# Six 512-column products ahead of one gate product in a one-core hybrid attention and RWKV layer

## The chip, the cores and the metric

The kernel runs on one core of a Trainium2 chip. What is measured is the device time of one execution in microseconds (us), and the comparison is between medians of repeated runs. TensorE (PE in the profile) multiplies, VectorE (DVE), ScalarE (ACT) and GpSimd (POOL) work elementwise, and SyncE (SP) issues the transfers. Each engine works through its own queue in order.

## The reference, cut to what matters

One layer over 512 tokens of width 1024: an input projection, a sparse attention (NSA) on half of the mixed width and an RWKV-7 recurrence on the other half, an output projection with residual, and a feed-forward part with squared ReLU. The change stands at the end of the RWKV half, where the normalised state output gets its bonus and is multiplied by a gate:

```python
def rwkv7_mixer(cols, ...):
    ...
    g = jax.nn.sigmoid(xg) @ g2
    ...
    y = wkv7_scan(rh, decay.reshape(B, T, H, N), kh, vh, -kk, kk * ah)
    ...
    y = ((y - mean) * lax.rsqrt(var + GN_EPS)).reshape(B, T, RWKV_WIDTH) * lnx_w + lnx_b
    bonus = jnp.sum(rh * kh * r_k, axis=-1, keepdims=True) * vh
    y = y + bonus.reshape(B, T, RWKV_WIDTH)
    return (y * g).astype(cols.dtype)
```

The matrix `g2` has 128 rows and 512 columns; the kernel holds it as the tile `G2P`, and sigmoid(xg) as `SG`.

## The kernel before

The 512 tokens are cut into four tiles of 128 (index `i`). Python generators stand for streams of work: the input projection (`rw_in`, `rw_v`, `nsa_in`), the RWKV steps of one tile (`rw_prep`, `rw_inv`, `rw_vals`), the recurrence over chunks (`rw_scan`), its output (`rw_outs`, which calls `rw_out(i)`), and the attention of one tile and head group (`attn_scores`, `attn_values`). `merge` takes turns among them by priority and by a modelled clock of its own, and so gives the order in which the program is written. The framework then plans the order of each engine's queue from modelled times (`schedule_with_timeline_sim=True`, line 1429), so instructions of neighbouring streams stand interleaved in the queues, and a plan made with more instructions need not keep the order of the rest.

The products of the input projection and of the feed-forward part go through `mm3` (lines 331 to 334), three products in single-pass form in place of one float32 product. Other products, among them the gate product, are plain float32; the profile records such a product as two TensorE instructions.

Results of TensorE land in PSUM banks. The tag `ps` has one bank, which `rw_out`, `rw_prep` and `rw_vals` share in turn: a tile of that tag can be written only when the reader of the one before is done. `pa` and `pb` have two banks each, `pi`, `pq` and `pz` one.

In `rw_out(i)` (lines 769 to 801) four transposes write `pty` (line 787), ScalarE reads it with scale and bias into `Y1` (line 792), GpSimd adds the bonus (line 794), the gate product of four 128-column pieces writes `pgt` in the same bank (line 797), and VectorE multiplies the two into `YR` (line 799). Around the first tile's gate product stand, on other streams: the triangular inverse of tile 1 (`rw_inv`: lines 694, 702, 712), its products with the state (lines 743, 752, 757), the preparation of tile 2 (`BK` at line 568, `pg` at line 586, read by VectorE at lines 589 and 590), the bonus of tile 1 (`rkp`, line 622) and the attention scores (`pcs` at line 1053, `sc` at line 1075, read by VectorE at lines 1058 and 1079 and by ScalarE at lines 1061 and 1082).

Of the kernel before, what the change touches and what calls it, by code (L numbers as in the profile page):

```python
# [114 lines left out]
def layer(ctx: ExitStack, tc: tile.TileContext, A, cst, out):  # L115
    nc = tc.nc
    PSUM = bass.MemoryType.PSUM
    V, S, G, PE = nc.vector, nc.scalar, nc.gpsimd, nc.tensor

    def bc(ap, shape):  # L120
        return ap.to_broadcast(shape)
# [54 lines left out]
    def at(place, shape, name, dt=F32):  # L176
        size, n = PLACES[place]
        assert int(np.prod(shape[1:])) * 4 <= size
        return up.tile(shape, dt, name=name, tag=place, bufs=n)
# [10 lines left out]
    def small(n, name):  # L190
        return sm.tile([128, n], F32, name=name, tag=name, bufs=1 if n == 32 else 2)
# [12 lines left out]
    ident = identr.bitcast(F32)  # L204
# [82 lines left out]
    def vec(key, j=0, n=1):  # L287
        return VEC[:, VO[key] + j:VO[key] + j + n]
# [10 lines left out]
    def rsqrt(v, n, key, p=128):  # L299

        y = small(n, "rs_y" + key)[0:p]
        G.tensor_tensor(y, v, bc(MH[0:p], [p, n]), op=ALU.pow)
        return y
# [27 lines left out]
    def mm3(o_, l, r, first, last):  # L331
        PE.matmul(o_, l[0], r[0], start=first, stop=False)  # L332
        PE.matmul(o_, l[0], r[1], start=False, stop=False)  # L333
        PE.matmul(o_, l[1], r[0], start=False, stop=last)  # L334

    def norm_T(i, x_, gain, NH_, NL_, place, pool, raw=None):

        ss = small(2, "ss")
        tmp = [at(place, [128, 512], "nt") for _ in range(2)]
        for b in range(2):  # L340
            S.activation(tmp[b], x_[b], AF.Square, scale=1.0 / 32, accum_out=ss[:, b:b + 1])
        vv = small(1, "vv")
        V.scalar_tensor_tensor(vv, ss[:, 0:1], 1e-6, ss[:, 1:2], op0=ALU.add, op1=ALU.add)
        rs = rsqrt(vv, 1, 'n')
        for b in range(2):
            V.scalar_tensor_tensor(tmp[b], x_[b], rs, gain[b], op0=ALU.mult, op1=ALU.mult)
            pt = pool([128, 4, 128], "pt")
            for kk in range(4):
                PE.transpose(pt[:, kk, :], tmp[b][:, kk * 128:(kk + 1) * 128], ident)
            S.copy(NH_[b][:, i], pt)  # L350
            if raw:
                S.copy(raw[b], pt)
            V.tensor_tensor(NL_[b][:, i], pt, NH_[b][:, i].bitcast(F32), op=ALU.subtract)
# [22 lines left out]
    G2P = at('c', [128, 4, 128], "G2P")  # L376
# [66 lines left out]
    def feat_cols(c0, use, halves=False):  # L443

        turn[0] ^= 1
        pas = [(pa_, pb_)[turn[0]]([128, T], "pa") for _ in range(2)]
        W = []
        for a in range(2 if halves else 1):
            i0, i1 = (2 * a, 2 * a + 2) if halves else (0, NT)
            for h in range(4):  # L450
                if a == 0:
                    W.append(piece(c0, h))
                hi, lo = W[h]
                for kk in range(2):
                    k = 2 * h + kk
                    for j in range(2):
                        js = slice(j * 128, (j + 1) * 128)
                        mm3(t4(pas[j])[:, i0:i1], (hi[:, kk, js], lo[:, kk, js]), xk(k, i0, i1), k == 0, k == KD - 1)
                    yield 1.3 * (i1 - i0) / NT, 0.0
        for j in range(2):  # L460
            use(j, pas[j])
# [307 lines left out]
    def rw_out(i):  # L769
        st = ST[i]  # L770
        YY = st['YY']
        mean = small(8, "mean")
        V.tensor_reduce(mean, YY, axis=AX.X, op=ALU.add)
        V.tensor_scalar(mean, mean, 1.0 / 64, None, op0=ALU.mult)
        V.tensor_tensor(YY, YY, bc(mean.unsqueeze(2), [128, 8, 64]), op=ALU.subtract)
        sq = at('o', [128, 8, 64], "sqy")
        S.activation(sq, YY, AF.Square)
        var = small(8, "var")
        V.tensor_reduce(var, sq, axis=AX.X, op=ALU.add)
        V.tensor_scalar(var, var, 1.0 / 64, 64e-5, op0=ALU.mult, op1=ALU.add)  # L780
        rs = rsqrt(var, 8, 'o')
        V.tensor_tensor(YY, YY, bc(rs.unsqueeze(2), [128, 8, 64]), op=ALU.mult)
        yield 0.0, 5.0
        pt = ps([128, 2, 2, 2, 64], "pty")
        for c in range(2):
            for p in range(2):
                PE.transpose(pt[:, c, p].rearrange("p a b -> p (a b)"),
                             YY[:, 4 * c + 2 * p:4 * c + 2 * p + 2, :].rearrange("p a b -> p (a b)"), ident)
        Y1 = at('o', [128, 4, 128], "Y1")
        for p in range(2):  # L790
            for e in range(2):
                S.activation(Y1[:, 2 * p + e, :].rearrange("p (c t) -> p c t", c=2), pt[:, :, p, 1 - e, :],
                             AF.Identity, bias=vec('lnb', 2 * p + e), scale=vec('lnw', 2 * p + e))
        G.tensor_tensor(Y1, Y1, st['ZV'], op=ALU.add)
        pgt = ps([128, 4, 128], "pgt")
        for kt in range(4):
            PE.matmul(pgt[:, kt, :], G2P[:, kt, :], SG[:, i * 128:(i + 1) * 128], start=True, stop=True)
        YR[i] = at('zk', [128, 4, 128], "YR")
        V.tensor_tensor(YR[i], Y1, pgt, op=ALU.mult)
        done['out', i] = 1  # L800
        yield 1.3, 0.0
# [8 lines left out]
    def rw_outs():  # L810
        for i in range(NT):
            yield lambda: ('chain', i) in done
            yield from rw_out(i)
# [22 lines left out]
    def tok_cols(c0, n, use):  # L836

        pas = [(pa_ if i < 2 else pb_)([128, 512], "pa") for i in range(NT)]
        for h in range(4):
            hi, lo = piece(c0, h)  # L840
            for kk in range(2):
                k = 2 * h + kk
                for i in range(NT):
                    mm3(pas[i][:, 0:n], xt(k, i), (hi[:, kk, :], lo[:, kk, :]), k == 0, k == KD - 1)
                    if i % 2:
                        yield 0.7, 0.0
        for i in range(NT):
            use(i, pas[i][:, 0:n])
# [331 lines left out]
    def outproj():  # L1180
        for i, b in OPO:
                yield lambda: ('n', i) in YS and ('r', i) in YS and ('wo', b) in done and all(z in done for z in GATE)
                Y2[i][b] = at(('zv', 'zr')[b], [128, 512], "y2")
                nc.sync.dma_start(Y2[i][b], A['x'][0, i * 128:(i + 1) * 128, b * 512:(b + 1) * 512])
                pa = pa_([128, 512], "pa")
                for k in range(KD):
                    y_ = YS['nr'[k // 4], i]
                    mm3(pa, (y_[0][:, k % 4, :], y_[1][:, k % 4, :]), WO[b, k], k == 0, k == KD - 1)
                V.tensor_tensor(Y2[i][b], Y2[i][b], pa, op=ALU.add)
                yield 5.2, 0.0  # L1190
                done['op', i, b] = 1
# [241 lines left out]
```

## Time and profile before

| | us |
|---|---|
| median of 3 runs | 785.54 |
| lowest and highest of the 3 | 783.43, 785.77 |
| the profiled execution | 783.81 |
| its span, first to last instruction | 781.9 |
| TensorE busy | 759.8 |
| VectorE busy | 511.8 |
| ScalarE busy | 395.6 |
| GpSimd busy | 175.2 |

The span is what the trace shows; 1.9 us of the profiled execution lie outside it. [...] A timeline row gives the start and the length of a group of instructions, their count, and in square brackets the idle time of the engine before them and what ended it. A row of the chain gives the time that a group put on the chain that ended last.

### The profile page before, as it was taken

Reading aid. Unit: us, or ns where it says so; the run is one execution under the profiler, and the core shown is the slowest. Engines: PE = TensorE matmul, PEld = TensorE weight load, DVE = VectorE, ACT = ScalarE, POOL = GpSimd, SP = SyncE. Lnnn points to the kernel's source line nnn. Section 1 sums busy time; section 2 is a strip of 40 time slices with the busy share of each in tenths; the row PEclk is TensorE's granted clock in tenths of the full one; section 3 lists DMA queues with packets and bytes.
Section 4 is the critical chain, followed back from the end, with each engine's and each line's share of the span. In section 5 each row is a group of like instructions: output and inputs, shape, how many; then the busy total and the mean of one; then the engine's idle time right before and its main releaser. Section 6 shows DMA issues by size and latency. Waiting matters only on the chain.

```text
span 781.9 us, 18278 instructions
## 1 busy us (share of the span) xinstructions
PE 759.8 (97%) x7357; PEld 657.5 (84%) x7357; DVE 511.8 (65%) x1157; ACT 395.6 (51%) x928; POOL 175.2 (22%) x176
## 2 busy tenths in 40 slices
PE   7999999999989999999999899999999999999998
PEld 5888888889879877887788899998888999978886
DVE  6444385585586789898755888973334989853333
ACT  7343433345444867888544655673332456653330
POOL 5002032240332353434400152300001323100000
PEclk9999999999985999999999999999999999999999
DMA  7741331111000000120343053233323433133212
GB/s 235 206 133 42 94 84 44 44 29 31 15 16 1 29 3 2 30 57 9 114 149 95 17 146 108 69 104 110 96 92 103 118 102 106 62 122 95 95 54 108
DMA packets 67338, 62.00 MB, mean 79 GB/s; under 512 B 6013, under 2 KB 53299, under 8 KB 67254
## 3 DMA queue, kind: packets, MB, share of 16 engines
q1 hardware_dynamic: 67254, 60.83, 25.9%
q8 instruction: 58, 0.95, 0.5%
q14 instruction: 26, 0.21, 0.1%
HBM read 58.72 MB, written 2.10 MB: 78 GB/s over the span
## 4 chain that ended last, share of the span: by engine, by line
PE 84%; DVE 7%; ACT 4%; DMA 3%; issue 1%; SPq 1%; POOL 0%; DVEq 0%; ACTq 0%; POOLq 0%
PE pa L332 8%; PE pa L333 8%; PE pa L334 8%; PE po L332 7%; PE po L333 7%; PE po L334 7%; PE pw L333 5%; PE pw L334 5%; PE pw L332 5%; PE pg L586 2%; PE sc L1075 2%; DMA wraw<-in_w_out_dram 1%; PE py L757 1%; PE pT L1111 1%; PE pz L681 1%
## 5 line engine op out<-in xcount | busy, mean ns | idle before, releaser
L311 ACT CAST whi<-wraw 128x512 fp32r<-128x512 f32 (+1 forms) x128 | 78.7, 622 | 133.4 <-PE po L333 29.1
L312 DVE TENSOR_TENSOR wlo<-wraw,whi 128x512 fp32r<-128x512 f32 (+1 forms) x120 | 86.7, 725 | 86.1 <-ACT whi L311 80.9
L332 PE MATMUL po<-whi 128*128 128x512 f32 x256 | 100.7, 394 | 1.2 <-DVE cc L1361 1.2
L333 PE MATMUL po<-wlo,whi 128*128 128x512 f32 x256 | 101.0, 395 | 0.0
L334 PE MATMUL po<-whi,wlo 128*128 128x512 f32 x256 | 100.7, 393 | 0.0
L333 PE MATMUL pw<-TT,whi 128*128 128x256 f32 x224 | 63.2, 282 | 0.0
L334 PE MATMUL pw<-TT,wlo 128*128 128x256 f32 x224 | 63.0, 281 | 0.0
L332 PE MATMUL pw<-TT,whi 128*128 128x256 f32 x224 | 62.5, 279 | 0.0
L332 PEld LDWEIGHTS po<-whi 128*128 128x128 f32 x256 | 48.0, 188 | 13.0 <-ACT whi L311 1.6
L334 PEld LDWEIGHTS po<-whi,wlo 128*128 128x128 f32 x256 | 48.1, 188 | 11.4
L333 PEld LDWEIGHTS po<-wlo,whi 128*128 128x128 f32 x256 | 48.0, 188 | 11.0
L332 PE MATMUL pa<-XH,whi 128*128 128x512 f32 (+1 forms) x144 | 53.0, 372 | 1.5 <-ACT XH L350 1.5
L333 PE MATMUL pa<-XL,whi 128*128 128x512 f32 (+1 forms) x144 | 53.7, 374 | 0.0
L334 PE MATMUL pa<-XH,wlo 128*128 128x512 f32 (+1 forms) x144 | 52.9, 370 | 0.0
L1291 POOL TENSOR_TENSOR ws<-wq 128x512 f32<-128x512 f32 x14 | 21.5, 1536 | 138.3 <-DMA wq<-in_w_ff_dram 123.2
L311 ACT CAST whi<-ws 128x512 fp32r<-128x512 f32 x56 | 33.0, 617 | 34.7 <-DVE ws L1296 9.5
L312 DVE TENSOR_TENSOR wlo<-ws,whi 128x512 fp32r<-128x512 f32 x56 | 48.2, 870 | 3.1 <-ACT whi L311 3.0
L1089 POOL TENSOR_SCALAR P<-P,z 128x128 f32<-128x128 f32 (+3 forms) x32 | 36.1, 1138 | 60.8 <-DVE z L1038 28.5
L312 DVE TENSOR_TENSOR wlo<-H,whi 128x512 fp32r<-128x512 f32 x32 | 22.1, 690 | 42.1 <-PE po L333 37.4
L334 PE MATMUL pw<-NH,wlo 128*128 128x256 f32 x168 | 47.0, 280 | 0.0
L333 PE MATMUL pw<-NL,whi 128*128 128x256 f32 x168 | 46.8, 279 | 0.0
L332 PE MATMUL pw<-NH,whi 128*128 128x256 f32 x168 | 46.8, 279 | 0.0
(317 smaller groups left out, 2007.9 us busy)
## 6 DMA issues: line engine op xcount, KB each, us to landing
wraw<-in_w_ff_dram SPq DMA_DIRECT2D x72, 256.0 KB
wq<-in_w_ff_dram SPq DMA_DIRECT2D x56, 256.0 KB
wraw<-in_w_in_dram SPq DMA_DIRECT2D x40, 256.0 KB
wraw<-in_w_in_dram SPq DMA_DIRECT2D x8, 268.0 KB
x<-in_x_dram SPq DMA_DIRECT2D x8, 256.0 KB
y<-in_x_dram SPq DMA_DIRECT2D x8, 256.0 KB
wraw<-in_w_out_dram SPq DMA_DIRECT2D x8, 256.0 KB
wraw<-in_w_out_dram SPq DMA_DIRECT2D x16, 128.0 KB
```

The costliest lines, as they stand in the source:

```text
L311: S.copy(hi, raw)
L312: eng.tensor_tensor(lo, raw, hi.bitcast(F32), op=ALU.subtract)
L332: PE.matmul(o_, l[0], r[0], start=first, stop=False)
L333: PE.matmul(o_, l[0], r[1], start=False, stop=False)
L334: PE.matmul(o_, l[1], r[0], start=False, stop=last)
L586: PE.matmul(pg[:, f], BK[ROW[e], 2 * f + c].rearrange("p a b -> p (a b)"), AR[c][ROW[e], f].rearrange("p a b -> p (a b)"), start=True, sto ...
L681: PE.matmul(o_[rows, b_, :], l[rows, b_, :], r[rows, b_, :], start=True, stop=True)
L757: PE.matmul(py[ROW[a], r, f, :], YL[e][c][:, f, a, :], uv, start=not q and f == 0 and e == 0, stop=True, skip_group_check=True)
L1075: PE.matmul(sc[:, h - h0, :], Qt[:, h, :], KT[br, g, hl].rearrange("p i t -> p (i t)")[:, 0:w], start=hl == 0, stop=hl == 1)
L1089: (G if (h, br) in SCG else V).tensor_scalar(P_[:, h, 0:w], P_[:, h, 0:w], z[:, h:h + 1], None, op0=ALU.mult)
L1111: PE.transpose(pt[:, h, :], P[br][:, h, j * 128:(j + 1) * 128], ident)
L1291: G.tensor_tensor(s3, q[0][0], q[1][0], op=ALU.subtract)
```

## The change

A helper `stir` writes `n` products of `l` and `r` to a PSUM tile, each as a group of its own. In `rw_out`, for the first tile alone, six of them go to `pgt`, with the identity as stationary operand and all 512 columns of `G2P` as the moving one. The gate product writes the same bank after them, so that nothing of theirs is read. They use no buffer of their own and issue no transfer.

```diff
+
+    def stir(o_, l, r, n):
+
+        for _ in range(n):
+            PE.matmul(o_, l, r, start=True, stop=True)
...
         pgt = ps([128, 4, 128], "pgt")
+        if i == 0:
+            stir(pgt, ident, G2P, 6)
         for kt in range(4):
             PE.matmul(pgt[:, kt, :], G2P[:, kt, :], SG[:, i * 128:(i + 1) * 128], start=True, stop=True)
```

## Rows read from the trace of the kernel before

**Rows 1.** The page: busy time by engine; granted clock in 40 slices; chain by engine.

```profile
PE 759.8 (97%) x7357; PEld 657.5 (84%) x7357; DVE 511.8 (65%) x1157; ACT 395.6 (51%) x928; POOL 175.2 (22%) x176
...
PEclk9999999999985999999999999999999999999999
...
PE 84%; DVE 7%; ACT 4%; DMA 3%; issue 1%; SPq 1%; POOL 0%; DVEq 0%; ACTq 0%; POOLq 0%
```

**Rows 2.** The span and mean granted TensorE clock of the core.

```profile
core 0: 781.9 us, clock 0.987
```

**Rows 3.** Stretches of TensorE: length, busy (instructions), granted clock, DMA share, GB/s.

```profile
230.00:230.50 0.50, 0.50 (x4) 0.71 0.01 4
230.50:231.00 0.50, 0.50 (x5) 0.50 0.00 0
...
250.50:251.00 0.50, 0.50 (x5) 0.81 0.00 0
251.00:251.50 0.50, 0.50 (x5) 1.00 0.00 0
```

**Rows 4.** TensorE timeline around the first gate product: start, length, group, idle before.

```profile
225.02 1.16 PE L797 MATMUL pgt<-SG,G2P 128*128 128x128 f32 x8 [0.20 <-ACT Y L792]
229.29 0.69 PE L702 MATMUL pz<-Tn,QU 32*32 32x32 f32 x32 [3.11 <-DVE Tn L694]
```

**Rows 5.** VectorE timeline of the same time, same columns.

```profile
226.86 2.05 DVE L622 SCALAR_TENSOR_TENSOR rkp<-r,VEC,k 128x128 f32<-128x128 f32 x4
228.83 0.41 DVE L694 TENSOR_TENSOR Tn<-Tn,pd 128x256 f32<-128x256 f32 x1
...
230.30 0.68 DVE L799 TENSOR_TENSOR YR<-Y,pgt 128x512 f32<-128x512 f32 x1
...
233.38 0.29 DVE L1079 CUSTOM_DVE_ANT_0 P<-sc,CT 128x128 f32<-128x128 f32 x1 [0.63 <-PE sc L1075]
...
235.39 0.42 DVE L589 TENSOR_TENSOR GA<-pg,CT 128x256 f32<-128x256 f32 x1 [1.07 <-PE pg L586]
...
238.28 0.29 DVE L1079 CUSTOM_DVE_ANT_0 P<-sc,CT 128x128 f32<-128x128 f32 x1 [1.97 <-PE sc L1075]
...
241.94 0.42 DVE L589 TENSOR_TENSOR GA<-pg,CT 128x256 f32<-128x256 f32 x1 [1.84 <-PE pg L586]
...
249.31 0.42 DVE L763 TENSOR_TENSOR Sn<-py,Sn 128x256 f32<-128x256 f32 x1 [2.13 <-PE py L757]
```

**Rows 6.** The chain, four pieces at 230 to 250 us: start, time, group.

```profile
229.98 1.61 PE pcs L1053 x8
231.59 1.76 PE sc L1075 x8
233.35 2.00 PE pg L586 x8
...
247.36 1.90 PE py L757 x32
```

**Rows 7.** The chain later, the same four products.

```profile
254.47 1.01 PE pcs L1053 x8
...
302.54 1.09 PE pg L586 x8
...
311.16 1.04 PE sc L1075 x8
...
324.50 1.11 PE py L757 x31
```

**Rows 8.** All engines from line 1053's first products to line 1075's eighth at 251.

```profile
229.98:251.07 21.09, 21.09 (x167) 19.45 (x166) 13.15 (x67) 10.88 (x48) 5.37 (x5) 0.51 0.01 2
```

**Rows 9.** The chain, the 512-column float32 product of line 534, twice.

```profile
204.97 0.43 PE pu L534
...
267.92 1.05 PE pu L534 x2
```

**Rows 10.** Waits of TensorE, one pair of lines: total, times, longest.

```profile
PE sc L1075 <- DVE mnc L1058: 1.1, 1, 1.1
```

## The prediction

> **What bounds the kernel now.** I read the page first, then the clock, then the timelines of the engines at the one place where the clock is low, then the chain. TensorE is busy for 97% of the span and holds 84% of the chain that ended last, so time on TensorE is worth looking at anywhere [rows 1]. The granted clock is full in 38 of 40 slices and drops in the 13th and 14th [rows 1]. [...]
>
> What TensorE did before the fall is in its timeline. The first tile's gate product ran from 225.02 to 226.18, then the engine stood idle for 3.11 us, until line 694's `Tn` let line 702 start at 229.29, and 0.9 us later the clock fell [rows 4]. That wait is VectorE's: `Tn` came behind the four `rkp` of 2.05 us, which began at 226.86 [rows 5]. The six products go into just this idle time.
>
> In the cold stretch TensorE is busy for all of its 21.09 us, VectorE for 13.15 and ScalarE for 10.88 [rows 8], and every piece of the chain from 229.98 to 251.07 is TensorE's; four of them are shown [rows 6]. So here a faster TensorE is worth something at once, until VectorE, whose own gaps are few, takes over.
>
> **The change part by part.** *The six products, on the path.* A float32 product of 512 columns is two instructions. In the chain line 534's second instruction took 0.43 us behind its first, and its pair 1.05 us between other products, which is 0.525 each [rows 9]. Six products are twelve instructions: 5.16 us by the one, 6.30 by the other. The twelve stand in one row with no other shape between, as the second instruction of line 534 does, so I take 0.43 and keep 0.525 for the range. They wait for the same bank as the gate product, so they start where that started, at 225.02; the gate product ends at 225.02 + 5.16 + 1.16 = 231.34, and line 702 starts then and not at 229.29 [rows 4]. So 3.11 of the 5.16 us lie in idle time, and 2.05 us are on TensorE's path (3.19 with the longer price).
>
> *VectorE behind them.* `YR` reads the gate product and stands in VectorE's queue at 230.30 [rows 5]. It now waits until 231.4, so everything queued behind it on VectorE, the score reductions of line 1079 and the masks of line 589 among them, is held by 1.1 us. Line 702 itself doesn't suffer from that, since `Tn` stands ahead of `YR` [rows 5].
>
> *The clock, gained.* With the products in place TensorE works from 225.02 on without the 3.11 us. If the clock then stays full, the pieces of the cold stretch run as they do elsewhere: the `pcs` of line 1053 in 1.01 us for 1.61, the `sc` of line 1075 in 1.04 for 1.76, the `pg` of line 586 in 1.09 for 2.00, the `py` of line 757 in 1.15 (31 of 32 in 1.11) for 1.90 [rows 6, 7]. Two `pcs`, two `sc`, three `pg` and the `py` are 14.8 us of the stretch and would be 8.5, a ratio of 0.575; all 21.09 us [rows 8] at that ratio are 12.1, so TensorE gains 9.0 us and after its own delay is 9.0 - 2.05 = 6.9 us ahead.
>
> *What is late next: VectorE.* Its gaps from 233 to 250 are 0.63, 1.07, 1.97, 1.84 and 2.13 us, 7.64 in all [rows 5]; with the 1.1 us of `YR` it can't be more than 6.5 us ahead. Not all gaps close at once. I follow the queues. TensorE: line 702 takes 0.69 us [rows 4], to 232.03, `pcs` to 233.04, the first `sc` to 234.08, `pg` to 235.17, line 712 (0.57 by the ratio, between the rows shown) and the second `sc` to 236.8, the next `pcs` and `pg` to 238.9. VectorE can start the first line 1079 group at about 234.15 (0.8 later than before), the first line 589 at 235.2 (0.2 earlier), the second 1079 group at 236.85 (1.4 earlier) and the second line 589 at 238.95 (3.0 earlier than 241.94). From there VectorE has work without a gap up to 247.19, where the 2.13 us before line 763 begin [rows 5]; that work now ends at 244.2, and line 763, whose product is there by 243.1, follows without a wait: 244.25 for 249.31, 5.06 us earlier. ScalarE and GpSimd keep ahead of that: in the stretch they are busy for 10.88 and 5.37 us [rows 8].
>
> *The rest of the kernel.* Behind 251 the work is started by engines and by buffers that they free, not by a clock, so what all of them are ahead stays. TensorE, 6.9 us ahead, waits for VectorE, which is 5.06 ahead; I count the smaller of the two. The sum against the profiled execution's own time is 783.81 - 5.1 = 778.7 us; that execution lies 1.73 us below the median of the three runs, so against the median it is 785.54 - 5.1 = 780.4 us.
>
> **The rivals.** *The clock falls all the same.* The stretch after line 702 stayed at half clock for 20.5 us though TensorE is busy in all of it [rows 3, 8], so this work did not bring the clock back for that long; at full clock its products are over sooner and leave more pauses. Then the clock falls some microseconds after 231, the stretch runs cold as before, and the products are on top. Against it: the same mix runs at full clock from 251 on, for the rest of the span [rows 1, 7], and a pause of TensorE of 1.1 us before a `sc` left it there [rows 10]. The time: 785.54 plus 2.05 to 3.19 us, 787.6 to 788.7, less what ran warm before the fall; I take 788. This is the case that ends slower. It decides by two things: that the clock falls before about 236, and that the instructions take more than about 0.46 us each (twelve of them then put over 2.36 us on the path, which is 0.3%). [...]
>
> *The gain is given back.* The clock stays full, but VectorE has no room for it: if `YR`'s 1.1 us and the changed meeting of VectorE and ScalarE leave only its two largest gaps closed (1.97 and 2.13, 4.1 us) and 1.1 plus a later wait of about 1 us are set against that, some 2 us are left: 783.5 us. For it speaks that VectorE is busy for 511.8 us of the span [rows 1]; against it, that the queues as followed above close more.
>
> *The queues are planned anew.* The plan is made from modelled times, and 5 us of new TensorE work change what is ready when. A different order behind 231 can cost or save; the one term of this sort that the rows price is an idle stretch of 3.11 us with a fall of the clock behind it, which cost 9.0 us of TensorE [rows 4, 8] and could come up elsewhere. Half of that size, to either side, is what I allow: 776 to 790 us.
>
> **How the numbers follow.** About 0.3% (2.36 us) is what a measurement of this kernel can tell from no change. The forecast, 780.4, has a chance of 0.58 and a range of its own of 778.5 (TensorE's 6.9 us in full) to 782.5 (the longer price of the products, 1.14 us, and one gap of about 1 us that stays open). The clock falls all the same: 0.20, half of it within 0.3% and half slower. Given back: 0.10, within 0.3%. Planned anew with an effect that outweighs the rest: 0.12, of it 0.05 faster, 0.02 the same, 0.05 slower. That makes faster 0.63, same 0.22, slower 0.15. The range that should hold 8 in 10 reaches from 777.5, a microsecond below the forecast's own range for the new plan, to 788.0, in the middle of the first rival.
>
> **What would show it.** Right: the granted clock at 1.0 throughout, a mean of 1.00; twelve instructions of line 339 (the helper's) of 0.43 us each from 225.0; line 702 at about 231.3; line 763 at about 244.3; the `pg` of line 586 at 1.1 us a group. The first step is wrong if the twelve take more than 5.5 us or don't start where the gate product started; the second if the clock falls between 231 and 251 after all; the third if the clock is full and line 763 still comes after 247; the last if the stretch is 5 us shorter and the end of the span isn't, which would show as a longer wait of TensorE or of a transfer behind 300. A fall of the clock at a place where there was none before would make the whole prediction wrong.

## The result and the profile after

The changed kernel is slower: a median of 796.79 us in four runs (793.75 to 798.09) against 785.65 us for the kernel before (783.43 to 787.72), a ratio of 1.0126 with a 95% interval of [1.0103, 1.015]. A ratio here compares fast executions alone, without the one slow execution among those below (`planned1`, 805.72 us), and need not be the quotient of two medians (1.0142). The forecast was 780.4 us with a range of 777.5 to 788.0, so the time lies outside the range and on the other side. The profiled execution took 798.09 us, with a span of 796.0 us against 781.9 [rows 2].

First the page of the kernel after (busy time by engine, granted clock in 40 slices) and its clock. The granted clock is a record of its own in the trace, as a share of the full clock, and TensorE counts as busy at whichever it is granted.

```profile
PE 771.9 (97%) x7369; PEld 665.5 (84%) x7369; DVE 513.2 (64%) x1157; ACT 396.0 (50%) x928; POOL 175.4 (22%) x176
...
PEclk9999999999996999999999999999999999999999
```

```profile
core 0: 796.0 us, clock 0.981
```

The drop of the clock is still there, one slice wide, and the mean clock has gone down where the forecast wanted 1.00: 0.019 of 796.0 us is 15.1 us of full clock lost, 4.9 more than the 10.2 of before (0.013 of 781.9 us [rows 2], the one piece of 20.5 us at half clock from about 230.2 to 250.7 [rows 3]). TensorE's idle time, span less busy, is 24.1 us for 22.1 before [rows 1, 2].

TensorE's timeline after, around the added products (start, length, group, idle before):

```profile
227.42 5.42 PE L339 MATMUL pgt<-G2P,identr 128*128 128x512 f32 x12 [0.19 <-ACT Y L797]
...
233.66 0.69 PE L707 MATMUL pz<-Tn,QU 32*32 32x32 f32 x32
...
237.37 1.06 PE L717 MATMUL px<-Tn,Z 32*32 32x32 f32 x32
239.08 1.97 PE L1082 MATMUL sc<-KT,QT 128*128 128x128 f32 x8 [0.65 <-DVE mnc L1065]
```

The products do what the change says: twelve instructions in 5.42 us, and line 707 (702 before) starts without the wait of 3.11 us [rows 4]. The clock is in stretches of the same engine (length, busy time and instructions, granted clock, DMA share, GB/s):

```profile
227.42:237.00 9.58, 9.58 (x75) 1.00 0.10 29
...
237.00:237.50 0.50, 0.50 (x9) 0.67 0.00 0
237.50:254.00 16.50, 15.85 (x117) 0.50 0.00 1
254.00:254.50 0.50, 0.50 (x5) 0.76 0.17 33
...
295.00:295.50 0.50, 0.50 (x5) 0.70 0.00 0
...
302.00:302.50 0.50, 0.50 (x6) 0.97 0.00 0
```

TensorE had no pause at all in the 9.58 us from its first product on, and at 237.2 the clock fell to 0.50 of full all the same, up to about 254.2. It fell again from 295.2 to 302.0, and twice more for 3.4 us, near 350 and 391, where the kernel before has no fall [rows 2, 3]. The page's slices don't show these: each is 19.9 us long, and 6.8 us at half clock, cut by a slice's edge, still reads 9.

TensorE's three largest waits between 255 and 400 us, first of the kernel before, then of the one after (what it waited for, total, times, longest):

```profile
PE pv L1124 <- ACT th L1115: 1.5, 2, 1.0
PE sc L1075 <- DVE mnc L1058: 1.1, 1, 1.1
PE pv L1128 <- DVE tl L1116: 0.7, 1, 0.7
```

```profile
PE pv L1131 <- ACT th L1122: 3.1, 3, 1.7
PE pv L1131 <- DVE YN L1145: 2.1, 1, 2.1
PE pv L1135 <- DVE tl L1123: 1.3, 4, 0.7
```

A wait of 2.1 us for line 1145's `YN`, VectorE's addition that reads the bank `pv` of one attention group before the next may write it, is new. It ends at 294.03, 1.2 us ahead of the second fall:

```profile
294.03 0.47 PE L1131 MATMUL pv<-th,VH 128*128 128x512 f32 x1 [2.06 <-DVE YN L1145]
```

The added products touch neither line, so something else has changed: the order of the queues. In the two traces the instructions of every engine, the products aside, come in the same order up to the place of the products. Behind it they differ on each engine: first on VectorE (at 230.0 us of the kernel before and 232.5 of the one after), on TensorE itself from 242.0 and 245.0 on, and in SyncE's queue loads of the output weights and of `y` have changed places. So the first fall, at 237.2, still stands behind TensorE instructions in the old order; those behind 251 don't. The experiments take order and products apart.

### The profile page after: what moved, and what is told of

Same layout as the page of the kernel before. It is cut to its first block, busy times and chain, and to the rows that moved or that the text cites. A ratio compares the mean times of both kernels' runs of the same rounds, so it can differ in the third digit from the quotient of the medians.

```text
span 796.0 us, 18310 instructions
## 1 busy us (share of the span) xinstructions
PE 771.9 (97%) x7369; PEld 665.5 (84%) x7369; DVE 513.2 (64%) x1157; ACT 396.0 (50%) x928; POOL 175.4 (22%) x176
## 4 chain that ended last, share of the span: by engine, by line
PE 75%; DVE 12%; ACT 5%; DMA 3%; issue 3%; POOL 1%; SPq 0%; DVEq 0%; ACTq 0%; POOLq 0%
PE pa L332 8%; PE pa L333 8%; PE pa L334 8%; PE po L332 7%; PE po L334 7%; PE po L333 7%; PE pw L333 3%; PE pw L334 3%; PE pw L332 3%; DVE wlo L312 2%; PE pg L591 2%; PE sc L1082 2%; ACT whi L311 2%; PE pT L1118 1%; DMA wraw<-in_w_ff_dram 1%
## 5 line engine op out<-in xcount | busy, mean ns | idle before, releaser
L334 PEld LDWEIGHTS po<-whi,wlo 128*128 128x128 f32 x256 | 48.1, 188 | 11.4
L312 DVE TENSOR_TENSOR wlo<-H,whi 128x512 fp32r<-128x512 f32 x32 | 22.1, 689 | 42.1 <-PE po L333 37.2
```

Of the source, the lines that this page charges most:

```text
L312: eng.tensor_tensor(lo, raw, hi.bitcast(F32), op=ALU.subtract)
```

## The experiments

Theory A: the new order of the queues costs the time, and the six products in the old order do about what was forecast. Theory B: the products cost it themselves, since they don't hold the clock and are on top. To hold an order, the program is planned twice: the order of every queue is read from the first plan, and in the second each two neighbours of a queue get an edge that orders them without a semaphore.

### The products in the order of before, and the order without the products

`pinned6` has the six products and the queues of before; `plan6_without` has the queues of the changed kernel and no products. Their traces show just these orders, on every engine.

```diff
+        for a, b in zip(row, row[1:]):     # row: one engine's queue, from the first plan
+            tc.add_manual_dep(b, a.name, no_sync, reason="queue order")
...
+    _, queues = program(arrays, args_in, 0)          # pinned6; 6 in plan6_without
+    nc, _ = program(arrays, args_in, 6, queues)      # pinned6; 0 in plan6_without
```

> The six products ahead of the first gate product, with every queue held in the order that it has in the kernel before (ordering edges without waits; the products stand directly ahead of the gate product). Theory A (the queues planned anew are the loss, the products do what was forecast): the clock stays full from 225 to 252, line 763's counterpart comes about 5 us earlier, 780.4 us. Theory B (the clock falls all the same, the products are on the path): a fall some microseconds after 231, about 20 us at half clock, 787 to 789 us. If the new order alone is the loss and the clock falls as well, this lies at 787 to 789 and not at 797.

> No added product, but every queue in the order that the changed kernel has. Leaves the six products out, computes the same. Theory A: the order is the loss, so most of the 11 us stays, 793 to 797 us. Theory B (products and clock are the loss, the order is neutral): 784 to 788 us, and the one fall of the clock at about 230 as before.

`plan6_without`: 795.42 us in four runs, a ratio of 1.0108 [1.0082, 1.0134] to 786.94 us before. `pinned6`: 785.52 us in ten runs, 0.9969 [0.9943, 0.9996]. So the order alone costs 8.5 us, and the six products in the old order, with the edges that hold it, cost nothing. Theory A holds for the sign and for most of the 11 us. Its other half, the gain, shows in three executions of ten (below); the median of 785.52 lies between the two times expected of `pinned6`.

The page and clock of `plan6_without`, and two rows of its TensorE timeline:

```profile
PE 767.4 (97%) x7357; PEld 664.9 (84%) x7357; DVE 512.8 (65%) x1157; ACT 396.1 (50%) x928; POOL 175.1 (22%) x176
```

```profile
core 0: 793.6 us, clock 0.978
```

```profile
231.45 0.69 PE L707 MATMUL pz<-Tn,QU 32*32 32x32 f32 x32 [3.13 <-DVE Tn L699]
...
293.25 0.47 PE L1131 MATMUL pv<-th,VH 128*128 128x512 f32 x1 [2.07 <-DVE YN L1145]
```

The idle stretch ahead of line 707 is back, as it must be without the products, and the wait for `YN` stands at the same place as after; the clock falls 0.5 us behind it, at 293.8. The ledger, each term from the page and the clock: 26.2 us idle (4.1 over before), 0.022 of 793.6 us or 17.5 us lost to the clock (7.3 over before), together 11.4. Between the spans lie 11.7 us, but line 707 starts 2.2 us later than before (231.45 for 229.29) behind the same idle stretch, a difference that stands ahead of the change (below); so the two terms stand for 9.5 us and are 1.9 too many. In the kernel after the same two are 2.0 and 4.9 us, and the products 5.42, together 12.3 for 14.1 us between the spans less 2.4 of the start, 11.7. The ledger names the terms and is good to about 2 us, not better. Part of the place can be seen too. Here are the stretches from the last `pv` to the end of the output projection, and in them the number of one of its three product kinds, of the kernel before and then of `plan6_without`:

```profile
397.60:434.17 36.57, 36.51 (x174) 1.00 0.35 108
```

```profile
L334 PE MATMUL pa<-whi,wlo 128*128 128x512 f32 x48 | 19.0, 398 | 0.0
```

```profile
403.46:444.61 41.15, 41.09 (x189) 1.00 0.27 84
```

```profile
L334 PE MATMUL pa<-whi,wlo 128*128 128x512 f32 x56 | 22.2, 396 | 0.0
```

Before, eight more triples of the projection stood ahead of the last `pv`, among attention work that leaves TensorE gaps (2.75 us idle of the 43.10 from 354.50 to 397.60 us); in the new order they come behind it, where TensorE has no gaps to fill (0.06 us idle in either stretch above), and the stretch is 4.6 us longer, while 4.13 us of the 43.66 ahead of it are idle. Whether the second fall follows from the wait for `YN`, or both from the changed meeting of the engines, these two runs don't separate.

In `pinned6` the clock was not the same in each execution. Three of ten had a mean of 0.997 to 1.0 and took 779.46 to 781.29 us, around the forecast of 780.4; seven had 0.987 to 0.993 and took 784.07 to 787.42. The kernel before, 25 times beside it, always had 0.982 to 0.987. The profiled execution is one of the seven (TensorE's timeline, then a stretch of all engines):

```profile
226.87 5.42 PE L339 MATMUL pgt<-G2P,identr 128*128 128x512 f32 x12 [0.19 <-ACT Y L797]
...
233.11 0.69 PE L707 MATMUL pz<-Tn,QU 32*32 32x32 f32 x32
```

```profile
239.50:249.00 9.50, 9.50 (x87) 8.47 (x86) 5.90 (x31) 5.67 (x27) 3.95 (x5) 0.50 0.01 3
```

The clock falls at 239.0, not 1 us behind line 707 as before but 6, and is back at 249.2: 10.2 us at half clock for 20.5, and one more piece of 3.4 us near 270 (mean clock 0.991). So 3.4 us of clock loss are gone and about 2 us of products are on the path, which is about why such executions (median 786.17) come out near the 786.94 of before. VectorE's timeline shows one thing that the forecast left out:

```profile
233.85 0.35 DVE L720 TENSOR_SCALAR QU<-Tn,CT 128x256 f32<-128x256 f32 x1 [1.88 <-PE pz L707]
234.12 0.68 DVE L806 TENSOR_TENSOR YR<-Y,pgt 128x512 f32<-128x512 f32 x1
```

Ahead of `YR` in VectorE's queue stands a `QU` that needs line 707's product. `YR` starts 7.25 us after the first product, where before it started 5.28 after the gate product [rows 4, 5]: it is held by 2.0 us, not by 1.1.

### Fewer and more products, in either order

`pinned3` and `pinned12` change the number in the old order; `planned3` and `planned1` change it with the queues planned anew.

```diff
-    nc, _ = program(arrays, args_in, 6, queues)
+    nc, _ = program(arrays, args_in, 3, queues)      # pinned3; 12 in pinned12
...
-            stir(pgt, ident, G2P, 6)
+            stir(pgt, ident, G2P, 3)                 # planned3, no queue order; 1 in planned1
```

> Three products in place of six, all queues in the order of before. They take 3 x 2 x 0.43 = 2.6 us and end with the gate product at 228.8, inside the idle time, so nothing is delayed. Theory A: clock stays full, TensorE about 9 us ahead, VectorE 6 to 7, 778 to 780 us. Theory B: the clock falls as before or some microseconds later, 783 to 786 us.

> Twelve products, all queues in the order of before: 10.3 us, the gate product ends at 236.5, line 702 is 7.2 us late. Theory A (the clock is held): 785.5 + 7.2 less about 9, 783 to 786 us, and 5 us above the run with six. Theory B (the clock falls after them in any case): 785.5 + 7.2, 792 to 794 us.

> The changed kernel with three products in place of six, the queues planned anew as in the change. With three products and the old queues the time was 784.35. Theory A (the plan is the loss, and it is the plan's luck, not the amount of TensorE work): the plan moves as much as with six, so the time may lie anywhere from 783 to 798; if it lies above 790 the loss belongs to planning anew at this place at all. Theory B (the amount of added work is what costs): within 1 us of the run with three products and the old queues, 783 to 786.

> The change with one product in place of six, the queues planned anew. One product is 0.9 us of TensorE inside the idle time, so its own cost is nothing. Theory A (the plan is the loss): the order after it differs from before's from the same place on, and the time is 790 to 800 as with three and six. Theory B (the amount is the loss): 784 to 787, as the kernel before.

| | runs | us | ratio to before |
|---|---|---|---|
| pinned3 | 10 | 784.35 | 0.9953 [0.9927, 0.9979] |
| pinned6 | 10 | 785.52 | 0.9969 [0.9943, 0.9996] |
| pinned12 | 10 | 789.34 | 1.0021 [0.9999, 1.0043] |
| planned1 | 4 | 795.49 | 1.0115 [1.0092, 1.0137] |
| planned3 | 4 | 800.49 | 1.0180 [1.0132, 1.0228] |
| after (planned with 6) | 4 | 796.79 | 1.0126 [1.0103, 1.015] |

One product, about 1 us of work, is enough to set off a new plan, and each of the three new plans is 1.1 to 1.8% slower with no relation to the number of products. In the old order the time goes up with the number: in the executions that kept the clock (three of ten each time) 777.7 to 779.2 with three products, 779.5 to 781.3 with six, 784.8 to 786.4 with twelve. On the mean of the three the last step is 5.2 us for six more products with nothing to hide them; the first is 2 us for three, of which the idle stretch still hides a part. The other executions took 783.9 to 785.9, 784.1 to 787.4 and 788.7 to 791.7 us. So the median of `pinned12` lies between its two theories, as that of `pinned6` did, and `planned3` lies 2.5 us above the widest range that was given for it.

All three new plans have a second fall of the clock next to a pause of TensorE, for different waits: the changed kernel's is told above, that of `planned1` comes at 298.7 us behind 1.5 us of waiting for `Tn`, that of `planned3` at 289.0 within 2.5 us of waiting for `mn`. So it isn't `YN` as such. That the pause brings the fall is likely by this, and not shown.

The profiled execution of `pinned3` kept the clock here, so it shows what the forecast was about: its clock, TensorE and VectorE around the products, a stretch of TensorE, its weight loads, VectorE, ScalarE, GpSimd, and the one later piece at half clock.

```profile
core 0: 777.3 us, clock 0.997
```

```profile
227.78 2.84 PE L339 MATMUL pgt<-G2P,identr 128*128 128x512 f32 x6 [0.19 <-ACT Y L797]
...
232.06 0.69 PE L707 MATMUL pz<-Tn,QU 32*32 32x32 f32 x32 [0.55 <-DVE Tn L699]
...
244.61 1.16 PE L591 MATMUL pg<-AR,BK 64*128 64x128 f32 x8
```

```profile
244.42 0.40 DVE L768 TENSOR_TENSOR Sn<-py,Sn 128x256 f32<-128x256 f32 x1
```

```profile
232.00:252.00 20.00, 19.95 (x268) 17.91 (x268) 19.10 (x94) 16.46 (x67) 5.93 (x6) 1.00 0.04 14
```

```profile
439.00:442.00 3.00, 3.00 (x15) 0.50 0.01 3
```

The same `pg` of the kernel before, the first behind its stretch at half clock:

```profile
251.00 1.16 PE L586 MATMUL pg<-AR,BK 64*128 64x128 f32 x8
```

From the start of line 702 to this `pg` 21.71 us pass before [rows 4], and 12.55 here (232.06 to 244.61): TensorE gains 9.16 us, where the forecast had 9.0. Line 768 (763 before) is 4.89 us earlier than before [rows 5], although the gate work began 2.76 us later (227.78 for 225.02): with that, 7.7 us. VectorE is now busy for 19.10 of 20 us, but TensorE is for 19.95, and the chain from 232.06 to 256 us is TensorE's alone: VectorE comes near to being the bound and doesn't become it. The last additions of the kernel, before and in `pinned3`, from VectorE's timeline:

```profile
773.30 5.55 DVE L1404 TENSOR_TENSOR y<-y,po 128x512 f32<-128x512 f32 x8 [5.74 <-PE po L334]
```

```profile
768.66 5.55 DVE L1411 TENSOR_TENSOR y<-y,po 128x512 f32<-128x512 f32 x8 [5.74 <-PE po L334]
```

They are 4.64 us earlier, with the later start 7.4 of the 9.16. The piece at half clock, 3.4 us from 438.7 on, takes 1.7 of what is missing; the kernel before has none there [rows 3].

### The idle stretch taken away without products

`tn_first` has no products; in VectorE's queue the last `Tn` of tile 1 goes ahead of the second `BK` of tile 2, everything else as before. `tn_first_pg1` has that too, and adds one product ahead of each of the next three `pg`.

```diff
+    what, to = text['Tn', 1, 4], text['BK', 2, 1]
+    for q in queues:
+        if what in q:
+            q.remove(what)
+            q.insert(q.index(to), what)
...
+                if i == 2:                            # n_pg: (0,0,0,0) in tn_first, (1,1,1,0) in tn_first_pg1
+                    stir(pg.rearrange("p f a b -> p (f a b)"), ident, G2P, n_pg[2 * c + e])
```

> No products. Queues of before but for one instruction: VectorE's Tn of line 694, which ended the idle 3.11 us, stands ahead of the second BK of line 568 and not behind rkp. TensorE can go on at 226.2. If the idle time is what the clock falls on, the clock is held in at least as many runs as with three products, and the 3 us come on top where TensorE leads: 777 to 782 in those runs. If the clock falls on the thin work after it in any case, it falls at 235 to 240 in most runs: 783 to 787.

> As the run with Tn first, and one product ahead of each of the three pg products of tile 2, 2.6 us in all. If it takes both, no idle time and some products in the thin stretch, the clock is held in most runs and the time is 777 to 781; if one of the two does it alone, this is within 1.5 us of the better of the two runs that have one of them.

`tn_first`: 783.41 us in nine runs, 0.9955 [0.9938, 0.9972], with a mean clock of 0.986 to 0.989 in all nine. TensorE's timeline and three stretches:

```profile
228.53 0.69 PE L717 MATMUL pz<-Tn,QU 32*32 32x32 f32 x32
...
233.11 1.90 PE L601 MATMUL pg<-AR,BK 64*128 64x128 f32 x8 [1.95 <-DVE YR L816]
```

```profile
233.00:233.50 0.50, 0.39 (x2) 0.76 0.00 0
233.50:250.00 16.50, 16.50 (x146) 0.50 0.01 2
250.00:250.50 0.50, 0.50 (x5) 0.67 0.00 0
```

The 3.11 us are gone, but `pg` takes the `ps` bank from the gate product, and now waits 1.95 us until `YR` has read it; the clock falls at 233.3 and is back at 250.3. The idle time was moved and shortened by 1.2 us, and the piece at half clock is 17.1 us long for 20.5, which is worth 1.7: together 2.9 of the 3.1 us that the median lies below before's 786.48. `tn_first_pg1`, 788.13 us in ten executions, 1.0014 [0.9993, 1.0035], lies outside both times that were expected of it, and its mean clock was 0.986 or 0.987 in all ten. Its first product waits the same 1.95 us for `YR`, and in its trace the clock falls at 232.0, before that product starts at 232.75 and takes 2.05 us, for 1.07 at full clock (`gate3_pg1`, below). So taking away the one idle stretch ahead of line 702 doesn't keep the clock, but neither run is without a pause here, and products behind the pause come too late to say what they would do ahead of it.

### Products spread over the stretch behind the gate

These three have the queues of before, a few products at the gate, and more ahead of the next `pg` of tile 2, in their bank.

```diff
-    nc, _ = program(arrays, args_in, 6, queues)                    # pinned6
+    nc, _, _ = program(arrays, args_in, 3, (2,2,2,0), queues)      # gate3_pg2
+    nc, _, _ = program(arrays, args_in, 3, (1,1,1,0), queues)      # gate3_pg1
+    nc, _, _ = program(arrays, args_in, 2, (1,1,0,0), queues)      # gate2_pg1
```

> Queues of before; three products ahead of the first gate product and two more ahead of each of the next three pg products of line 586 (tile 2), nine in all, into the bank that those write. If the clock falls near 239 because the products there do not hold it, the six further on hold it in nearly every run: mean clock 1.00 in most, and the time is that of three products with a held clock (about 778) plus what of the six (5.2 us) TensorE has no room for, it being about 2 us ahead of VectorE: 779 to 783. If the clock falls all the same in most runs: 787 to 791.

> Queues of before; three products ahead of the first gate product and one ahead of each of the next three pg products, six in all as in the change. With two ahead of each pg (nine in all) most runs kept a mean clock of 0.997 to 1.00 and took 783.3. If one each holds the clock as well, 2.6 us of TensorE work are saved and the time is 780 to 781.5; if one each is too little, the clock falls in most runs as with three products alone and the time is 784 to 787.

> Queues of before; two products ahead of the first gate product and one ahead of each of the next two pg products, four in all. If what the products have to do is fill the idle 3.11 us and little more, the clock is held as often as with six and the time is 779 to 780.5; if the clock falls in most runs, 783 to 786.

| | runs | us | ratio to before | mean clock |
|---|---|---|---|---|
| gate3_pg2 | 10 | 783.26 | 0.9963 [0.9937, 0.9989] | 0.996 or more in 8 of 10, 0.993 and 0.994 in two |
| gate3_pg1 | 12 | 781.51 | 0.9957 [0.9933, 0.9981] | 0.997 or more in 10 of 12 |
| gate2_pg1 | 4 | 791.83 | 1.0078 [1.0061, 1.0096] | 0.982 in all |

`gate3_pg2` ends 0.3 us above what was expected of it. `gate3_pg1` is 0.4% faster than the kernel before, clear of noise, but its interval overlaps those of `pinned3` and of `tn_first`, which has no products and lost the clock each time, so it isn't shown to be faster than those two. Its ten executions with the clock took 779.82 to 782.89 us, the other two 788.43 and 790.20. Its TensorE timeline and a stretch of TensorE:

```profile
226.73 2.84 PE L339 MATMUL pgt<-G2P,identr 128*128 128x512 f32 x6 [0.19 <-ACT Y L799]
...
233.47 1.07 PE L339 MATMUL pg<-G2P,identr 128*128 128x512 f32 x2
```

```profile
230.00:256.00 26.00, 25.46 (x309) 1.00 0.04 12
```

`gate2_pg1`, with fewer, lies outside what was expected of it. Its timeline and stretch:

```profile
231.22 0.69 PE L709 MATMUL pz<-Tn,QU 32*32 32x32 f32 x32 [1.41 <-DVE Tn L701]
...
235.16 2.02 PE L339 MATMUL pg<-G2P,identr 128*128 128x512 f32 x2
```

```profile
232.50:255.50 23.00, 23.00 (x162) 0.50 0.01 2
```

An idle stretch of 1.41 us is left ahead of line 709, the clock falls at about 232.1, and the products behind it then run at half clock: 2.02 us for 1.07. They lengthen the stretch that they should have kept short, to 23.9 us.

## Why the prediction was wrong, and where it was right

**The step that failed: "the rest of the kernel".** The sum costed the edit inside the queues of before and let "what all of them are ahead" stay to the end, as if the queues stayed too. The case "planned anew" had the mechanism, but a chance of 0.12 and half of one known stall as its size, up to 4.5 us (its range joins 4.5 below the forecast to 4.5 above the kernel before). The order alone cost 8.5 us (1.0108). What mis-sized it: the one stall priced there was 9.0 us of TensorE, and a new order doesn't move one such place but all that follow, here through a second fall of the clock near 295, further short ones, 4.1 us more idle time and projection work that no longer fills gaps. That three different additions gave three slower plans says that for this kernel the case was the likeliest, not one in eight; three plans are too few to say that a new plan is always worse.

**The second: "the clock, gained".** In the kernel after the clock fell at 237.2 though the products had closed the idle time, and the piece at half clock was still 17.1 us long for 20.5; in the old order the clock was kept in three of ten executions. The first rival, given 0.20, was the commoner one. Its price was too high: 787.6 to 788.7 us, with the whole stretch at half clock; such executions took 784.07 to 787.42 with six products, beside a kernel before of 786.94, since the stretch began later and was 10.2 us long instead of 20.5. The argument against this rival, that the same mix runs at full clock behind 251, was weak: the rows behind 251 say what the clock does with one order only. In the trace after the clock fell four times, three of them behind 251, and two of these about 1 us behind pauses of 2.06 and 1.7 us; but the fall at 237.2 had none in the 9.58 us up to 237.00, and that a pause brings a fall no run here shows.

**Right: the price of the products.** Forecast 5.16 us for twelve instructions, measured 5.42; line 707 starts 6.24 us after the first product in the kernel after, for 6.32 by the sum. At half clock the price doubles (2.02 us a product in `gate2_pg1`, for 1.07 in `gate3_pg1`), which the sum had no term for.

**Right where the clock is kept and the order too: the gain on TensorE.** 9.16 us measured in `pinned3`, with three products, for 9.0, and "given back" did not happen there. *What is late next: VectorE* is not borne out: its 5.06 us, the smaller term and the one that was counted, would be 7.1 without the products' 2.05 on the path, and 7.4 us arrived at the end though a further fall of the clock took 1.7; the chain stayed TensorE's. That the three executions of `pinned6` at 779.5 to 781.3 us meet the forecast of 780.4 is in part luck: beside them the kernel before took 786.94 and not 785.54, so they gained about 6.1 us (median 780.83) where 5.1 was forecast and TensorE's term alone was 6.9.

**The signs to look for** named a fall of the clock at a new place as what would make the whole prediction wrong; that is what the trace after shows, at 295.

## What to carry to other kernels

Where a planner sets the order of the queues, compare the order of the two programs before costing an added instruction, and judge an edit with the old order held: here an instruction pair of 1 us set off a new plan, and the kernel came out 1.1% slower. Products that keep the clock pay only while it is kept: with three of six spread through the thin stretch it was kept in 10 of 12 executions (`gate3_pg1`, 781.51 us), with the six in one block ahead of it in 3 of 10 (`pinned6`, 785.52 us), and behind a fall they cost double (2.02 us for 1.07). Even where the clock is kept, set their price against it: `tn_first`, with one VectorE instruction moved and no products, has a ratio of 0.9955 to before, within noise of the best of them. Read the mean clock beside the slices of the page: a slice that reads 9 can hide several microseconds at half clock (6.8 us over two slices in the kernel after).

## What the runs showed of the hardware that was not expected

One and the same program doesn't get the same clock each time: `pinned6` kept it in 3 of 10 executions, `gate3_pg1` in 10 of 12, and before in none of its 65 beside these runs. What differs between them, the runs don't show.

A TensorE without a pause was not safe from a fall, and not soon out of it: no pause in the 9.58 us up to 237.00 of the kernel after, which fell at 237.2, and 23.00 us busy throughout at 0.50 in `gate2_pg1`, from 232.50 to 255.50.

At the start the record of the clock doesn't match the durations. The first rows are of the kernel after, timeline and stretch, the others of the one before; the queues are the same there:

```profile
13.74 1.91 PE L354 MATMUL pt<-identr,nt 128*128 128x128 f32 x8
```

```profile
13.50:16.00 2.50, 2.50 (x13) 1.00 0.70 237
```

```profile
13.57 1.03 PE L349 MATMUL pt<-identr,nt 128*128 128x128 f32 x8
```

```profile
13.50:16.00 2.50, 2.50 (x24) 1.00 0.87 292
```

Eight transposes take 1.91 us in the one execution and 1.03 in the other, both under a record of 1.00. It puts 2.4 us between two executions ahead of anything that the change touches, which is why a single profiled execution should not be compared with another by its span alone.
